# Seven block products for eight in six of ten projections, with 1024-token blocks and a second stage read back from DRAM

## The chip, the cores and the metric

The kernel runs on one core of one Trainium2 chip. Its engines work side by side, each on its own queue of instructions in a fixed order: PE (matmuls, with its weight loads shown apart as PEld), DVE (elementwise work), ACT (copies, casts, activation functions), POOL (small operations and the DMAs of its own queue) and SP (which here only issues DMAs). SBUF is the memory that the engines work on, PSUM holds matmul results in eight banks of 128 x 512 float32, and DRAM holds inputs, outputs and intermediate tensors. The metric is the time of one execution in microseconds on the device; less is better.

## What is computed

One decoder block on x of 2048 tokens x 1024 channels, all float32. The normed input is projected onto nine parts, two token mixers work on them, and two branch products, gates and an output product follow. Cut to what matters:

```python
xn = rms_norm(x, g_pre)
proj = xn @ w_in      # r_x, r_z, m_x, m_z, m_o, m_i, m_f, gate_r, gate_m
u = causal_dwconv(r_x, rg_conv_w, rg_conv_b)
h_r = rg_lru(u, headwise(u, rg_w_a) + rg_b_a, headwise(u, rg_w_x) + rg_b_x, rg_lambda)
y_r = h_r * silu(r_z)
c = silu(causal_dwconv(m_x, ml_conv_w, ml_conv_b))
q, k, v = heads(c @ w_q), heads(c @ w_k) / 16, heads(m_x @ w_v)    # 4 heads of 256
h_m = sigmoid(m_o) * mlstm_chunkwise(q, k, v, i_pre, logf)         # chunks of 128 tokens
y_m = (layer_norm(h_m) * ml_norm_g + ml_skip * c) * silu(m_z)
y = sigmoid(gate_r) * (y_r @ w_branch_r) + sigmoid(gate_m) * (y_m @ w_branch_m)
out = x + rms_norm(y @ w_out, g_post)
```

The ten large products, each 2048 x 1024 x 1024, are those of r_x, r_z, m_x, m_z, m_o, gate_r, gate_m, the two branches and w_out. `rg_lru` is a linear recurrence along the tokens, and `mlstm_chunkwise` carries a 256 x 256 state from chunk to chunk.

## The kernel before

Each float32 operand is split into a high part (a cast to the matmul's narrower format, on ACT) and a low part (the difference, on DVE). Each product is the sum of three matmuls, high x high, high x low and low x high. `wtile` (lines 215 to 226) does that for a weight tile of 128 x 1024 that SP has loaded into `raw`: `whi` by line 223, `wlo` by line 225; three buffers hold each. `split` (line 250, 253) does it for 128 x 512 activations, `stage_a2` (145, 146) for the transposed input. `mm3` (232 to 234) issues the three matmuls of one 128 x 128 weight piece, and `gemm` does so for eight pieces, 24 matmuls into one PSUM bank.

The tokens are worked through in four blocks of 512. `stage_a` loads and norms a block of x and `stage_a2` transposes it on PE (line 142), so that channels lie on the partitions. `block` then runs, for each of eight channel tiles: `rx` (projection, `conv`), the recurrence's gates, `rz`, and the R branch's gate, and after them the R branch's products (`branch_mm`). Then, for each of four heads, `ogate`, the M projections (`Head.x`, `Head.z`), values and queries (`v`, `q`), and the chunks, which are placed between the matmuls of the next head's projections by hooks. The M branch's gates and products follow, then `stage_f` with w_out. Each weight is loaded and split once in each block, four times in all. Activations between the stages stay in SBUF, in a pool of 60 slots of 128 x 512 float32 (`t2k`).

The order on each engine's queue is made when the program is built: a list scheduler goes by the place in the program's text, moves up what is ready when an engine would idle by its own clock, and lets the blocks under `high_priority` go ahead, those of `wtile` by 200 places. The waits between the engines are put in afterwards. On the chip each queue then runs strictly in that order.

The lines that the prediction's steps use: 134 (scaling of x), 142 to 146 (transpose and split of x), 223 and 225 (weight split), 232 to 234 (matmuls), 258 to 265 (`conv`), 292/293 and 486/487 (silu), 307 to 334 (the recurrence), 347 (`branch_mm`), 365 to 367 (`ogate`), 509 to 515 (values), 537 to 582 (keys, weights, state split), 603 to 612 (chunk), 633 (skip scaling), 644/647 (`back`), 759 to 778 (output).

Of the kernel before, what the change touches and what calls it, by code (L numbers as in the profile page):

```python
# [13 lines left out]
P = 128  # L14
# [5 lines left out]
NK = D // P  # L20
H = 4
# [4 lines left out]
SW = 1152  # L26
# [6 lines left out]
def hybrid_kernel(ctx: ExitStack, tc: tile.TileContext, x, w_ch, w_mo, w_gate, w_q, w_k, w_v, w_out,  # L33
# [80 lines left out]
    def stage_a(b):  # L114
# [8 lines left out]
        for t in range(NT):  # L123
            for q in range(2):
                junk = t2k("junk")
                if q and b == 0:
                    nc.vector.scalar_tensor_tensor(out=junk, in0=xh[t][q], scalar=1.0 / D, in1=xh[t][q],
                                                   op0=ALU.mult, op1=ALU.mult, accum_out=ss[:, t, q:q + 1])
                else:
                    nc.scalar.activation(out=junk, in_=xh[t][q], func=AF.Square, scale=1.0 / 32.0,  # L130
                                         accum_out=ss[:, t, q:q + 1])
            rstd = rms_scale(ss[:, t, :])
            for q in range(2):
                nc.vector.tensor_scalar(out=xh[t][q], in0=xh[t][q], scalar1=rstd, scalar2=None, op0=ALU.mult)
        return xh

    def stage_a2(xh, ks=range(NK)):
        hl = []
        for k in ks:
            ps = psum()  # L140
            for t in range(NT):
                nc.tensor.transpose(ps[:, t * P:(t + 1) * P], xh[t][k // 4][:, (k % 4) * P:(k % 4 + 1) * P], ident)
            hi = t2k("xhi", F32R)
            lo = t2k("xlo", F32R)
            nc.scalar.activation(out=hi, in_=ps, func=AF.Copy, scale=vcol(V_GPRE, k))
            last = nc.vector.scalar_tensor_tensor(out=lo, in0=ps, scalar=vcol(V_GPRE, k), in1=f32(hi),
                                                  op0=ALU.mult, op1=ALU.subtract)
            hl.append((hi, lo))
        xdone[0] = last.ins
        return hl  # L150

    with tc.high_priority():
        xT = stage_a2(stage_a(0))
# [37 lines left out]
    qk_raw = []  # L191

    def late_setup():
        nc.sync.dma_start(out=gpost_t, in_=gpost)
        for h in range(H):
            q2 = t2k("q2")
            k2 = t2k("k2")
            nc.sync.dma_start(out=q2, in_=w_q[h])
            nc.sync.dma_start(out=k2, in_=w_k[h])
            qk_raw.append((q2, k2))  # L200


    def combine_qk(h):
        q2, k2 = qk_raw[h]
# [10 lines left out]
    def wtile(width, parts):  # L215
        hi = wp.tile([P, SW], F32R, tag="whi", name=nm("whi"), bufs=3)
        lo = wp.tile([P, SW], F32R, tag="wlo", name=nm("wlo"), bufs=3)
        raw = wp.tile([P, 1056], F32, tag="raw", name=nm("raw"), bufs=RAWB)
        nw[0] += 1
        with tc.high_priority(offset=WPRI if nw[0] > 3 else 0):  # L220
            for dst, src in parts(raw):
                nc.sync.dma_start(out=dst, in_=src)
            nc.scalar.copy(out=hi[:, :width], in_=raw[:, :width])  # L223
            eng = nc.gpsimd if 1 < nw[0] < 4 else nc.vector
            eng.tensor_tensor(out=lo[:, :width], in0=raw[:, :width], in1=f32(hi)[:, :width], op=ALU.subtract)  # L225
        return hi, lo

    def wchan(i):
        return wtile(1024, lambda r: [(r[:, :1024], w_ch[i])])

    def mm3(ps, lt, rt, first, last):
        mmul(ps, lt[0], rt[0], start=first, stop=False)  # L232
        mmul(ps, lt[0], rt[1], start=False, stop=False)  # L233
        mmul(ps, lt[1], rt[0], start=False, stop=last)  # L234

    def gemm(i, rhs, hooks=None):
        whi, wlo = wchan(i)
        ps = psum()
        for k in range(NK):
# [645 lines left out]
```

## Time and profile before

| | us |
|---|---|
| median of 3 runs | 2118.42 (2117.47 to 2119.43) |
| the profiled execution | 2117.8 |
| its span, first to last instruction | 2116.0 |
| granted PE clock over it | 0.999 |

A row of a group reads: line, engine, operation, output<-inputs with sizes, count | busy us, mean ns of one | idle time of the engine just before them and what ended it. A row of the waits reads: who waited for whom: us in total, times, longest. A row of the timeline reads: start, duration, engine, line, operation. A row of the windows reads: from:to, length, then busy us (and count) of PE, PEld, DVE, ACT and POOL, granted clock, the DMA engines' share, GB/s. A row of the DMA issues ends with count, size of one and the median time from issue to landing. The slices of busy tenths, each 52.9 us, over the whole span:

```profile
PE   7999999999999999999999999999999999999998
PEld 5888899888888889988888888998888888999887
DVE  6567587856467748885546775887545677588653
ACT  4567355434356635553335754555333584455432
POOL 2010000000110100000011000000001100000000
```

The four blocks are seen as four repeats of ten slices in the row of DVE.

### The profile page before, as it was taken

Reading aid. Unit: us, or ns where it says so; the run is one execution under the profiler, and the core shown is the slowest. Engines: PE = TensorE matmul, PEld = TensorE weight load, DVE = VectorE, ACT = ScalarE, POOL = GpSimd, SP = SyncE. Lnnn points to the kernel's source line nnn. Section 1 sums busy time; section 2 is a strip of 40 time slices with the busy share of each in tenths; the row PEclk is TensorE's granted clock in tenths of the full one; section 3 lists DMA queues with packets and bytes.
Section 4 is the critical chain, followed back from the end, with each engine's and each line's share of the span. In section 5 each row is a group of like instructions: output and inputs, shape, how many; then the busy total and the mean of one; then the engine's idle time right before and its main releaser. Section 6 shows DMA issues by size and latency. Waiting matters only on the chain.

```text
span 2116.0 us, 28070 instructions
## 1 busy us (share of the span) xinstructions
PE 2089.7 (99%) x10880; PEld 1792.1 (85%) x10880; DVE 1397.2 (66%) x2323; ACT 1032.8 (49%) x1683; POOL 162.5 (8%) x318
## 2 busy tenths in 40 slices
PE   7999999999999999999999999999999999999998
PEld 5888899888888889988888888998888888999887
DVE  6567587856467748885546775887545677588653
ACT  4567355434356635553335754555333584455432
POOL 2010000000110100000011000000001100000000
PEclk9999999999999999999999999999999999999999
DMA  5322322232343232223234233222324422322223
GB/s 198 100 101 88 117 70 80 80 120 90 118 151 103 92 107 81 70 77 124 89 130 154 86 100 100 72 78 70 131 92 131 149 88 97 100 71 80 80 90 119
DMA packets 82133, 215.57 MB, mean 102 GB/s; under 512 B 8112, under 2 KB 28848, under 8 KB 82000
## 3 DMA queue, kind: packets, MB, share of 16 engines
q1 hardware_dynamic: 77968, 202.01, 29.3%
q0 software_dynamic: 3744, 11.64, 1.6%
q8 instruction: 85, 1.39, 0.3%
q14 instruction: 48, 0.39, 0.1%
q10 hardware_dynamic: 288, 0.13, 0.0%
HBM read 204.28 MB, written 9.47 MB: 101 GB/s over the span
## 4 chain that ended last, share of the span: by engine, by line
PE 95%; DVE 2%; issue 1%; ACT 1%; DMA 1%; POOL 0%; DVEq 0%; SPq 0%; POOLq 0%
PE ps L232 24%; PE ps L233 24%; PE ps L234 24%; PE ps L366 3%; PE ps L365 3%; PE ps L367 3%; PE ps L770 3%; PE ps L771 3%; PE ps L772 3%; PE ps L563 1%; PE ps L511 1%; PE ps L510 1%; PE ps L509 1%; PE ps L642 1%; PE ps L547 1%
## 5 line engine op out<-in xcount | busy, mean ns | idle before, releaser
L225 DVE TENSOR_TENSOR wlo<-raw,whi 128x1024 fp32r<-128x1024 f32 x334 | 408.7, 1224 | 378.1 <-ACT whi L223 376.9
L223 ACT CAST whi<-raw 128x1024 fp32r<-128x1024 f32 (+1 forms) x336 | 352.6, 1049 | 591.3 <-PE ps L233 255.1
L232 PE MATMUL ps<-xhi,whi 128*128 128x512 f32 x1536 | 600.0, 391 | 0.0
L233 PE MATMUL ps<-xlo,whi 128*128 128x512 f32 x1536 | 598.8, 390 | 0.0
L234 PE MATMUL ps<-xhi,wlo 128*128 128x512 f32 x1536 | 598.5, 390 | 0.0
L234 PEld LDWEIGHTS ps<-xhi,wlo 128*128 128x128 f32 x1536 | 288.5, 188 | 60.8
L232 PEld LDWEIGHTS ps<-xhi,whi 128*128 128x128 f32 x1536 | 288.8, 188 | 56.1
L233 PEld LDWEIGHTS ps<-xlo,whi 128*128 128x128 f32 x1536 | 288.7, 188 | 55.7
L265 DVE SCALAR_TENSOR_TENSOR u<-cv,vecs,u 128x512 f32<-128x512 f32 x192 | 143.9, 749 | 5.3
L365 PE MATMUL ps<-whi,xhi 128*128 128x256 f32 (+1 forms) x512 | 146.9, 287 | 0.0
L367 PE MATMUL ps<-whi,xlo 128*128 128x256 f32 (+1 forms) x512 | 145.4, 284 | 0.0
L366 PE MATMUL ps<-wlo,xhi 128*128 128x256 f32 (+1 forms) x512 | 145.0, 283 | 0.0
L347 DVE SCALAR_TENSOR_TENSOR tg<-tg,ps 128x512 f32<-128x512 f32 x64 | 43.8, 685 | 100.0 <-PE ps L234 100.0
L232 PE MATMUL ps<-yrh,whi 128*128 128x512 f32 x256 | 101.3, 396 | 0.9 <-ACT yrh L250 0.9
L233 PE MATMUL ps<-yrl,whi 128*128 128x512 f32 x256 | 100.0, 391 | 0.7 <-DVE yrl L253 0.7
L232 PE MATMUL ps<-ymh,whi 128*128 128x512 f32 x256 | 100.4, 392 | 0.0
L770 PE MATMUL ps<-whi,yh 128*128 128x512 f32 x256 | 99.9, 390 | 0.0
L234 PE MATMUL ps<-yrh,wlo 128*128 128x512 f32 x256 | 99.8, 390 | 0.0
L234 PE MATMUL ps<-ymh,wlo 128*128 128x512 f32 x256 | 99.7, 390 | 0.0
L772 PE MATMUL ps<-whi,yl 128*128 128x512 f32 x256 | 99.6, 389 | 0.0
L233 PE MATMUL ps<-yml,whi 128*128 128x512 f32 x256 | 99.6, 389 | 0.0
L771 PE MATMUL ps<-wlo,yh 128*128 128x512 f32 x256 | 99.6, 389 | 0.0
(227 smaller groups left out, 3566.7 us busy)
## 6 DMA issues: line engine op xcount, KB each, us to landing
raw<-in_w_ch_dram SPq DMA_DIRECT2D x256, 512.0 KB, 3.5
raw<-in_w_out_dram SPq DMA_DIRECT2D x32, 512.0 KB, 3.4
raw<-in_w_mo_dram SPq DMA_DIRECT2D x24, 512.0 KB, 3.9
xh<-in_x_dram SPq DMA_DIRECT2D x32, 256.0 KB, 5.8
xr<-in_x_dram SPq DMA_DIRECT2D x32, 256.0 KB, 4.2
out_dram<-o POOLq DMA_DIRECT2D x24, 256.0 KB, 3.2
raw<-in_w_mo_dram SPq DMA_DIRECT2D x8, 528.0 KB, 3.4
graw<-in_w_gate_dram SPq DMA_DIRECT2D x16, 256.0 KB, 3.7
```

Of the source, the lines that this page charges most:

```text
L223: nc.scalar.copy(out=hi[:, :width], in_=raw[:, :width])
L225: eng.tensor_tensor(out=lo[:, :width], in0=raw[:, :width], in1=f32(hi)[:, :width], op=ALU.subtract)
L232: mmul(ps, lt[0], rt[0], start=first, stop=False)
L233: mmul(ps, lt[0], rt[1], start=False, stop=False)
L234: mmul(ps, lt[1], rt[0], start=False, stop=last)
L265: nc.vector.scalar_tensor_tensor(out=u, in0=cv[:, q:q + 512], scalar=vcol(wbase + q, j), in1=u, op0=ALU.mult, op1=ALU.add)
L365: mmul(o, xh[:, sl], whi[:, ws], start=ki == 0, stop=False)
L366: mmul(o, xh[:, sl], wlo[:, ws], start=False, stop=False)
L367: mmul(o, xl[:, sl], whi[:, ws], start=False, stop=ki == NK - 1)
L770: mmul(pt, y[ki][0][:, s], whi[:, ws], start=ki == 0, stop=False)
L771: mmul(pt, y[ki][0][:, s], wlo[:, ws], start=False, stop=False)
L772: mmul(pt, y[ki][1][:, s], whi[:, ws], start=False, stop=ki == NK - 1)
```

## The change

**Seven products for eight.** For the six projections that read x (r_x, r_z, gate_r, m_x, m_z, gate_m) the kernel now works on superblocks of 1024 tokens. x is cut in two along the tokens and in two along the contraction (a11, a12, a21, a22, each 512 x 512), and a pair of channel tiles with the same halves of the contraction forms b11, b12, b21, b22. The seven products are, with s1 = a21 + a22, s2 = s1 - a11, s3 = a11 - a21, s4 = a12 - s2: a11 b11, a12 b21, s4 b22, a22 (b21 - (b22 - (b12 - b11))), s1 (b12 - b11), s2 (b22 - (b12 - b11)), s3 (b22 - b12). Products are accumulated in PSUM where their sums allow it; three sums of a pair are made by DVE out of a bank and a copy. A pair's third and fourth product run after the first four of the next pair.

**X.** `build_first` and `build_second` make seven split sets of x, of 4 x 2 slots each, 56 slots of a pool of 74. Both run at the start of the kernel for superblock 0; for superblock 1 they run at the end of the second stage of superblock 0.

**Weights.** Tiles are 128 x 512 now, in four buffers each for whi and wlo and six raw ones. The R branch loads its weights once for two blocks.

**Two stages.** `phase_a` runs, for p = 0 to 3, the six pairs of the projections, the recurrence, and two o gates of head p (one for each block). It writes yr, mx, c, mz, the branch gates gr and gm, and th to DRAM by POOL's queue. `phase_b` reads them back by SP's queue, splits yr, ym, mx and c there, and runs the heads, the branches and w_out, with hooks for the chunks in the R and M branches; the chunks of the last two heads stand ahead of half of w_out for the first block. ym and the R branch's result go through DRAM too.

**Small parts.** `conv` takes the three columns of the block before by five small POOL operations and one small addition on DVE, its first term moves to ACT; the skip scaling moves to ACT; the last block's output no longer goes tile by tile behind PE, and its stores go by POOL's queue; the memory reserved for POOL's DMA descriptors is 4096 bytes a partition.

The diff, cut to its core:

```diff
-SW = 1152
+SW = 576
+KH = NK // 2
+    def build_second(xh1, raw, X):
+        for kk in range(KH):
+            a11, a12 = raw["a11", kk], raw["a12", kk]
+            a21 = xraw(xh1, kk, "a21")
+            a22 = xraw(xh1, kk + KH, "a22")
+            X["a22"].append(split(a22, "a22"))
+            s1 = t2k("s1r")
+            tt = nc.vector.tensor_tensor
+            tt(out=s1, in0=a21, in1=a22, op=ALU.add)
+            X["s1"].append(split(s1, "s1"))
+            tt(out=s1, in0=s1, in1=a11, op=ALU.subtract)
+            X["s2"].append(split(s1, "s2"))
+            tt(out=a21, in0=a11, in1=a21, op=ALU.subtract)
+            X["s3"].append(split(a21, "s3"))
+            tt(out=a12, in0=a12, in1=s1, op=ALU.subtract)
+            X["s4"].append(split(a12, "s4"))
...
+    with tc.high_priority():
+        raw0 = build_first(load_norm(0), XS)
+        build_second(load_norm(1), raw0, XS)
...
+    def early():
+        nw[0] += 1
+        return tc.high_priority(offset=WPRI if nw[0] > 2 else 0)
+    class Pair:
...
+            with early():
+                b11 = wraw(512, w_ch[n1][:, 0:512])
+                b21 = wraw(512, w_ch[n1][:, 512:1024])
+                b12 = wraw(512, w_ch[n2][:, 0:512])
+                b22 = wraw(512, w_ch[n2][:, 512:1024])
+                f = slice(0, 512)
+                W[1] = wsplit(b11, 512)
+                W[2] = wsplit(b21, 512)
+                tt(out=b11[:, f], in0=b12[:, f], in1=b11[:, f], op=ALU.subtract)
+                W[5] = wsplit(b11, 512)
+                tt(out=b11[:, f], in0=b22[:, f], in1=b11[:, f], op=ALU.subtract)
+                W[6] = wsplit(b11, 512)
+                tt(out=b12[:, f], in0=b22[:, f], in1=b12[:, f], op=ALU.subtract)
+                W[7] = wsplit(b12, 512)
+                W[3] = wsplit(b22, 512)
+                tt(out=b21[:, f], in0=b21[:, f], in1=b11[:, f], op=ALU.subtract)
+                W[4] = wsplit(b21, 512)
+        def a(self):
+            self.x_ = psum()
+            self.prod(self.x_, 1, "a11", True)
+            m1 = t2k("m1")
+            nc.scalar.copy(out=m1, in_=self.x_)
+            z = psum()
+            self.prod(z, 2, "a12", True)
+            self.cons.add(0, 0, z, m1)
+            self.y_ = psum()
+            self.prod(self.y_, 5, "s1", True)
+            self.m5 = t2k("m5")
+            nc.scalar.copy(out=self.m5, in_=self.y_)
+            self.prod(self.x_, 6, "s2", False)
+            self.v = t2k("v")
+            nc.scalar.copy(out=self.v, in_=self.x_)
+        def b(self):
+            self.prod(self.x_, 7, "s3", False)
+            self.cons.add(1, 1, self.x_, self.m5)
+        def c(self):
+            self.prod(self.y_, 3, "s4", False)
+            self.cons.add(0, 1, self.y_, self.v)
+            self.prod(self.x_, 4, "a22", False)
+            self.cons.plain(1, 0, self.x_)
...
+    def gemm(i, ys, hooks=None):
+        ps = [psum() for _ in ys]
+        for c in range(2):
+            whi, wlo = wload(512, w_ch[i][:, c * 512:(c + 1) * 512])
+            for kk in range(KH):
+                k = c * KH + kk
+                s = slice(kk * P, (kk + 1) * P)
+                for n in range(len(ys)):
+                    mm3(ps[n], (whi[:, s], wlo[:, s]), ys[n][k], k == 0, k == NK - 1)
+                if hooks and k in hooks:
+                    hooks[k]()
...
+                pr = Pair(g, p, X, cons)
+                pr.a()
+                d, defer[:] = list(defer), []
+                if prev:
+                    prev.c()
+                for f in d:
+                    f()
+                pr.b()
+                prev = pr
...
+        for u in range(8):
+            b, h = 2 * sb + u // 4, u % 4
+            hd.s1(G)
...
+            if u < 4:
+                hd.s2()
+                for m in range(2):
+                    br(2 * h + m, hooks[m])
+            elif u < 6:
+                if u == 4:
+                    st["ym"] = loads(Q["ym"][0], "ym")
+                    st["y"] = []
+                hd.s2()
+                for m in range(4):
+                    bm(0, 4 * (u - 4) + m, {3: lambda m=m: hd.chunk(m)})
+            else:
+                hd.s2()
+                for c in range(NT):
+                    hd.chunk(c)
+                out_half(2 * sb, st["y"], u - 6, st)
+            hd.norm()
...
-NSLOT = 60
-RAWB = 3
+NSLOT = 74
+RAWB = 6
-VEB = 1
+WB = 4
```

More of the change, by code (lines that the diff above doesn't have):

```diff
@@ L135, in stage_a, with split @@
         return xh
[L137 to L150, printed above, removed]
+    def split(src, name, eng="a"):
+        hi = t2k(name + "h", F32R)
+        lo = t2k(name + "l", F32R)
+        nc.scalar.copy(out=hi, in_=src)
+        nc.vector.tensor_tensor(out=lo, in0=src, in1=f32(hi), op=ALU.subtract)
+        return hi, lo
@@ L212, in combine_qk @@
         nc.gpsimd.dma_start(out=gq_d[h], in_=g2)
[L215 to L218, printed above, removed]
-        nw[0] += 1
[L220 to L226, printed above, removed]
@@ L228, in wchan @@
-    def wchan(i):
-        return wtile(1024, lambda r: [(r[:, :1024], w_ch[i])])
-    def mm3(ps, lt, rt, first, last):
[L232 to L239, printed above, removed]
-            sl = slice(k * P, (k + 1) * P)
-            mm3(ps, (whi[:, sl], wlo[:, sl]), rhs[k], k == 0, k == NK - 1)
-            if hooks and k in hooks:
-                hooks[k]()
-        return ps
@@ new lines, in wsplit, with wload @@
+    def wsplit(raw, width):
+        hi = wp.tile([P, SW], F32R, tag="whi", name=nm("whi"), bufs=WB)
+        lo = wp.tile([P, SW], F32R, tag="wlo", name=nm("wlo"), bufs=WB)
+        nc.scalar.copy(out=hi[:, :width], in_=raw[:, :width])
+        nc.vector.tensor_tensor(out=lo[:, :width], in0=raw[:, :width], in1=f32(hi)[:, :width], op=ALU.subtract)
+        return hi, lo
+    def early():
+        nw[0] += 1
+        return tc.high_priority(offset=WPRI if nw[0] > 2 else 0)
+    def wload(width, src):
+        with early():
+            return wsplit(wraw(width, src), width)
@@ L518, in q @@
             chl = self.chl
-            whi, wlo = self.wqv
             self.qs = []
@@ new lines, in branch, with fetch, loads @@
+    def branch(i, d, ys, tgs, dsts):
+        def fetch(src, name):
+            t = t2k(name)
+            nc.sync.dma_start(out=t, in_=src)
+            return t
+        with early():
+            tg = [fetch(s, "tgl") for s in tgs]
+        pb = gemm(i + d, ys, dsts.get("hooks"))
+        for n, t in enumerate(tg):
+            nc.vector.scalar_tensor_tensor(out=t, in0=t, scalar=1.0, in1=pb[n], op0=ALU.add, op1=ALU.mult)
+        return tg
+    def loads(src, name):
+        out_ = []
+        for k in range(NK):
+            t = t2k(name)
+            with early():
+                nc.sync.dma_start(out=t, in_=src[k])
+            out_.append(split(t, name))
+        return out_
```

620 lines of the change are left out of this document (328 added, 292 removed).

## The prediction

> **What bounds the kernel now.** I read the page first: busy shares, slices, the chain, the costliest groups.
>
> ```profile
> span 2116.0 us, 28070 instructions
> PE 2089.7 (99%) x10880; PEld 1792.1 (85%) x10880; DVE 1397.2 (66%) x2323; ACT 1032.8 (49%) x1683; POOL 162.5 (8%) x318
> PE 95%; DVE 2%; issue 1%; ACT 1%; DMA 1%; POOL 0%; DVEq 0%; SPq 0%; POOLq 0%
> L225 DVE TENSOR_TENSOR wlo<-raw,whi 128x1024 fp32r<-128x1024 f32 x334 | 408.7, 1224 | 378.1 <-ACT whi L223 376.9
> L223 ACT CAST whi<-raw 128x1024 fp32r<-128x1024 f32 (+1 forms) x336 | 352.6, 1049 | 591.3 <-PE ps L233 255.1
> ```
>
> PE works through 99% of the span and carries 95% of the chain. ACT's weight cast idles 255.1 us until PE gives a weight buffer back: the preparation waits for PE, not PE for it. The waits of PE alone confirm that; the columns are total us, times, longest:
>
> ```profile
> PE ps L142 <- DVE xh L134: 17.2, 6, 12.2
> PE ps L232 <- ACT yrh L250: 0.9, 3, 0.3
> PE ps L233 <- DVE yrl L253: 0.7, 3, 0.2
> ```
>
> Outside the transposes of x (L142) PE loses 1.6 us. A busy PE need not be at its peak, so I take its pace from the timeline, start to start:
>
> ```profile
> 599.74 0.39 PE L232 MATMUL ps<-xhi,whi 128*128 128x512 f32 x1
> ...
> 605.86 0.39 PE L232 MATMUL ps<-xhi,whi 128*128 128x512 f32 x1
> ```
>
> 27 steps lie between these rows: 6.12/27 = 0.2267 us for 512 columns, not the 0.39 of one record. Only fewer matmuls shorten this kernel, and that is what the change offers.
>
> **What goes.** Six projections are 6 x 8 channel tiles x 4 token blocks x 8 x 3 = 4608 matmuls. After: 48 pairs of seven products of 4 x 3 = 84, or 4032. The 576 that go are worth 576 x 0.2267 = **130.6 us**. No other matmul goes: the four remaining products keep their terms.
>
> **What is added on DVE**, by the nearest durations:
>
> ```profile
> L253 DVE TENSOR_TENSOR cl<-u,ch 128x512 fp32r<-128x512 f32 x32 | 21.9, 685 | 5.4 <-ACT ch L250 5.4
> L134 DVE TENSOR_SCALAR xh<-xh,rstd 128x512 f32<-128x512 f32 x32 | 18.1, 613 | 4.7 <-POOL rstd L88 4.7
> L265 DVE SCALAR_TENSOR_TENSOR u<-cv,vecs,u 128x512 f32<-128x512 f32 x192 | 143.9, 749 | 5.3
> L331 DVE TENSOR_TENSOR_SCAN hr<-a,hst,u 128x512 f32<-128x512 f32 x32 | 40.9, 1278 | 0.0
> L603 DVE SCALAR_TENSOR_TENSOR cst<-cst,dec,ps 128x258 f32<-128x258 f32 x120 | 53.2, 477 | 0.0
> L250 ACT CAST ch<-u 128x512 fp32r<-128x512 f32 x32 | 19.8, 619 | 16.1 <-DVE u L479 12.3 <-DVE lf L391 3.8
> L262 DVE TENSOR_SCALAR u<-cv,vecs 128x512 f32<-128x512 f32 x64 | 34.8, 543 | 0.7 <-ACT cv L259 0.7
> L146 DVE SCALAR_TENSOR_TENSOR xlo<-ps,vecs,xhi 128x512 fp32r<-128x512 f32 x32 | 22.2, 739 | 0.0
> L633 DVE TENSOR_SCALAR u<-u,sk 128x512 f32<-128x512 f32 x32 | 14.6, 479 | 0.0
> ```
>
> A 512-column half costs 0.685, more than half of 1.224. Projection weights: 48 pairs x 11 (seven splits, four differences) x 0.685 = 361.7 in place of 192 x 1.224 = 235.0, so +127. Three sums a pair: 144 x 0.685 = +99. The R branch loads its weights for two blocks at once: 32 halves for 32 whole tiles, 21.9 - 39.2 = -17. The other 112 whole tiles become 224 halves, +16, and the o gate forms 16 differences, +11. X: 2 x 44 operations x 0.685 = 60.3 for 23.6, +37. A convolution loses the 0.543 and gains a short add (0.16 as the small rows go): 64 x -0.38 = -25. The skip scaling moves to ACT, -15; half the gate-weight splits go, -6. Sum +227: 1397 + 227 = 1624 us of a span near 2070, 78%. ACT gains 144 copies and 24 more casts and copies of X a superblock at about 0.6, some 130 us: 1033 to about 1170, 56%. Neither is the bound on average, so I charge neither in full; PE's matmuls hide them. It is the stages that decide.
>
> First stage, one p: six pairs x 84 x 0.2267, two o gates and four recurrences' gates on PE. An o gate's matmul takes 0.12 us start to start (24 steps in 2.88):
>
> ```profile
> 783.08 0.28 PE L365 MATMUL ps<-whi,xhi 128*128 128x256 f32 x1
> ...
> 785.96 0.28 PE L365 MATMUL ps<-whi,xhi 128*128 128x256 f32 x1
> ```
>
> PE 114.3 + 2 x 96 x 0.12 + 24 x 0.2267 = 142.7. DVE: 84 operations in the pairs 57.5; eight convolutions at 3 x 0.75 + 0.16, 19.3; u splits 2.7; four gates at 3.33 with the scan, 13.4; silu work 10.9; o gates 6.9; gate weights 0.7: 111, or **78%**.
>
> Second stage, one superblock: eight heads of DVE 27.8 each (from the same kinds of rows: splits 5.5, keys 1.9, state splits 2.8, weights and queries 4.1, chunks 4.1, state 3.8, norm 2.7, back 2.9), 222; R branch 33; M branch 16 x 3.43 = 55; ym 11; output 45; gate scalars 14: 380. PE: heads 8 x 19.3, R 87, M 87, output 87 = 415. That is **92%**, and where the next X is built, 40 more, 420 of about 422. The stage nearest to it in the trace is the head loop of before:
>
> ```profile
> 310.00:500.00 190.00, 189.37 (x1067) 165.60 (x1066) 139.81 (x260) 90.64 (x171) 10.87 (x24) 1.00 0.28 92
> 850.00:865.00 15.00, 15.00 (x88) 13.27 (x87) 14.06 (x31) 6.53 (x13) 1.89 (x6) 1.00 0.21 70
> ```
>
> The third number is PE, then weight loads, DVE, ACT. There PE was full with DVE at 74% over 190 us and at 94% over 15 us. (Durations overstate by the overlap of neighbours, so my 92% is rather 85 to 90.)
>
> **Waits that are added.** (a) *Weight ring.* Before, three buffers of 24 matmuls (5.44 us each). After, four of 12 (2.72 us), and W3, W4 of a pair stay parked until the next pair has run its products 1, 2, 5, 6: two rotate. From release to the next use: cast 0.62, difference 0.69, hand-overs, drain 0.17, about 1.6 of 2.72 us, where before two buffers, 10.9 us, lay ahead. Behind a late cast stand the evacuations on ACT, behind a late difference the sums on DVE. Below: 0, as PE's waits of before. Above: two more operations ahead of each, 1.3 us on half of 336 products, 220 us. (b) *Slots.* X holds 56 of 74; 18 remain for the recurrence, whose three late u with their splits, gates, copies and stores come to about 18 when the R gate's pair ends. I take **25 us** for (a) and (b), three a p: the scheduler of before left PE 1.6, so it lies near the lower end. (c) *DRAM.* ym, yr, mx, c, z, th and the branch gates now go out on POOL's queue and back on SP's:
>
> ```profile
> raw<-gq_d SPq DMA_DIRECT2D x16, 256.0 KB, 3.1
> gq_d<-g POOLq DMA_DIRECT2D x4, 256.0 KB, 2.7
> ```
>
> 2.7 + 3.1 + a split of 1.3 is 7.1 us for a tile that is wanted at once. Early loads hide most; the last head's ym before the M branch, yr at the start of the stage and the slots for the next head do not all hide, with DVE at its 92%. Between 0 and 16 heads x 7.1 = 114 I take **40 us**, some 2.5 a head, below the middle, as before hid the same path for gq_d. SP's loads stand behind weight loads that wait for a raw buffer. In bytes, 2 x 288 tiles add 151 MB and the weights lose 59: about 150 GB/s; the 405 in the last column below, from the start of before, shows the room.
>
> ```profile
> 20.00:22.70 2.70, 2.42 (x12) 2.42 (x13) 2.70 (x5) 2.46 (x5) 0.00 (x0) 1.00 1.01 405
> 22.70:24.20 1.50, 1.50 (x6) 1.27 (x6) 1.50 (x4) 0.96 (x2) 0.00 (x0) 1.00 0.60 232
> ```
>
> **Ends.** Start: before, PE ran dense from 24.1.
>
> ```profile
> 12.19 3.83 PE L142 MATMUL ps<-ident,xh 128*128 128x128 f32 x16 [12.19 <-DVE xh L134]
> 22.75 0.78 PE L232 MATMUL ps<-xhi,whi 128*128 128x512 f32 x1
> 24.11 0.40 PE L232 MATMUL ps<-xhi,whi 128*128 128x512 f32 x1
> 15.16 5.06 DVE L134 TENSOR_SCALAR xh<-xh,rstd 128x512 f32<-128x512 f32 x2
> 14.29 3.16 POOL L225 TENSOR_TENSOR wlo<-raw,whi 128x1024 fp32r<-128x1024 f32 x1 [1.73 <-ACT whi L223]
> ```
>
> Two blocks of x must land, and 36 DVE operations of the second build (25 us) follow the second. That ends near 49 us; until then PE does products 1, 2 and part of 5, 6, 7 (11.5 us): dense as if from 37, **+14** (0 to 25). End: all four banks finish together; DVE's four rounds of 2.1 us no longer hide behind PE, and the stores leave by POOL: **+5** (3 to 8).
>
> ```profile
> 2108.51 0.60 ACT L777 ACTIVATE junk<-ps 128x512 f32<-128x512 f32 x1 [2.03 <-PE ps L772]
> 2110.96 1.41 DVE L759 SCALAR_TENSOR_TENSOR o<-o,rstd,xr 128x512 f32<-128x512 f32 x2 [0.66 <-POOL rstd L88]
> ```
>
> **Sum** against the profiled run, 2117.8 us (span 2116.0, the median of three is 2118.4): 2117.8 - 130.6 + 25 + 40 + 14 + 5 = **2071 us**, -2.2%.
>
> **Rivals.** *The stalls stay hidden*, as nearly all did before: 2117.8 - 130.6 + 19 = 2006. For it: PE's 1.6 us. Against it: every margin shrank. *DRAM is late at each head* (114 for 40): 2145, slower. For it: 92% on DVE and slots that are all taken. (After the start's idle PE's first three steps took 1.36 us in place of 0.68, so each such gap may cost 0.7 more, 11 us in all: 2156. The Trainium skill, page "TensorE: Matmul & The Clock Gate", section "Why this matters for your kernels", warns of a halved clock after gaps of over about 3 us. The granted clock stood at 1.00 in those steps, row 22.70 above, so the trace does not bear the mechanism out, and no weight is on it here.) *The weight ring starves PE*, on the other side: the place is the split ahead of each of the 336 products, the price up to 220 for 25, 2266. It decides from (130.6 - 19 - 40)/336 = 0.21 us a product. For it: ACT sat idle 255 us at this very cast and blocked what stood behind it; against it: 1.1 us of slack. *POOL holds DVE up:*
>
> ```profile
> L258 POOL COPY cv<-halo x64: 180/187/1167, 5.1 to 1909.5; 128x3 f32<-128x3 f32 x64
> ```
>
> A copy of three columns takes 187 ns as a median but up to 1167 (minimum, median, maximum), and DVE's L134 above took 5.06 us for two, at 0.61 a piece elsewhere, beside POOL's 3.16. The change makes six POOL operations of two in each of 64 convolutions: 256 x 0.19 = 49 us if each stops DVE and DVE is the bound, 2120, no change. The Trainium skill, page "SBUF — State Buffer", section "Who interferes with whom", says that a DVE instruction with two SBUF inputs contends with a GpSimd instruction that reads SBUF, whoever is first blocking the other; nearly all new DVE work is of that form. These rows agree. By that rule alone the 49 us would be the price; I give it little, since at 78% DVE in that stage has room.
>
> That the change does less than it says can't be: the matmuls are counted off the loops.
>
> **Chances.** Forecast (2025 to 2110) 0.45; hidden 0.20; DRAM 0.10; ring 0.14; POOL 0.05; 0.06 in between, mostly above. Faster by over 0.2%: 0.66; within 0.2%, about what a measurement of this kernel can tell from no change: 0.05; slower: 0.29. Eight in ten: below 2003 I leave 0.05, above 2190 some 0.14.
>
> **What would show it.** Right: 10304 matmuls, DVE near 1600 us or less by its page sum, PE's spacing unchanged at 0.227, PE idle near 100 us in all (ends included). Gaps of PE ahead of products, released by wlo or whi, are (a); ahead of ym, yr or mx splits, or behind DMA, (c); ahead of X's splits at the first 50 us, the start. The DVE share of the second stage against 92% tests the table. The prediction is wrong if PE's idle time exceeds 130 us or one of the stages runs at DVE's pace.

## The result, and the profile after

The changed kernel takes 2499.19 us (median of 4, 2496.11 to 2500.39) against 2118.49 for the one before: a ratio of **1.1795 [1.1775, 1.1815]**, 18% slower where 2.2% faster was forecast. The profiled execution took 2496.1 us. Its page, the busy times:

```profile
span 2494.3 us, 30483 instructions
PE 2094.7 (84%) x10304; PEld 1746.7 (70%) x10304; DVE 1608.4 (64%) x2941; ACT 1194.2 (48%) x2183; POOL 507.5 (20%) x868
```

The 576 matmuls are gone, and DVE (1608 us, forecast 1624) and ACT (1194, forecast 1170) carry what was worked out. Neither of the two got a larger share than forecast (64% for 78%, 48% for 56%): PE got emptier, from 99% to 84%, and its clock slower, from a mean of 0.999 to 0.917. The waits of PE (who waited for whom: us in total, times, longest) say where:

```profile
PE ps L258 <- DVE z L323: 114.2, 24, 17.7
PE ps L258 <- ACT ymh L137: 50.6, 10, 13.4
PE ps L571 <- DVE ex L564: 43.8, 4, 19.4
PE ps L646 <- ACT mxh L137: 32.4, 9, 6.6
...
PE ps L258 <- issue: 19.4, 6, 4.4
PE ps L258 <- ACT tr L435: 17.4, 7, 2.5
...
PE ps L495 <- ACT whi L245: 6.7, 7, 1.2
```

All rows of this view sum to 385.6 us, where before they summed to 18.8. Without any new loss the profiled run would have been 2117.8 - 130.6 = 1987.2, so 508.9 us were lost: 367 of them are waits by this view, and some 142 are the half clock and short waits that it doesn't name. PE's busy time bears that out: 2094.7 where 2089.7 - 130.6 = 1959.1 was due, 135.6 more. Three windows show the stages (from:to, length, then busy us and count of PE, PEld, DVE, ACT and POOL, granted clock, DMA share, GB/s): the first stage of the second superblock, then the two second stages, cut at the first matmul of each:

```profile
1290.95:1967.14 676.19, 600.07 (x2892) 500.76 (x2890) 443.88 (x721) 356.27 (x582) 198.69 (x322) 0.94 0.30 103
747.98:1290.95 542.97, 443.80 (x2246) 369.22 (x2247) 359.32 (x745) 238.31 (x506) 50.28 (x94) 0.90 0.44 150
1967.14:2481.66 514.52, 426.60 (x2182) 358.23 (x2182) 327.11 (x676) 207.40 (x440) 45.23 (x85) 0.91 0.45 151
```

The forecast's table had 571 us of PE for four p's and 415 for a second stage. So this first stage lost 105 us and the second stages 128 (with the next x's transposes) and 100, though DVE was busy there for only 66% and 64% of the time.

Of the waits, those for weights (last row) hardly count; z is the largest. It is the sum (1,1) of R's Z pair, which DVE must make out of PE's bank before product 4 may add to that bank. First a window in one such wait:

```profile
490.00:500.00 10.00, 0.55 (x3) 0.12 (x1) 5.58 (x7) 7.33 (x9) 0.96 (x1) 0.65 0.07 26
```

Then DVE's timeline in it (start, duration, line, operation; in brackets how long it waited and for whom):

```profile
491.00 0.69 DVE L246 TENSOR_TENSOR wlo<-raw,whi 128x512 fp32r<-128x512 f32 x1 [2.64 <-ACT whi L245]
492.15 0.69 DVE L450 SCALAR_TENSOR_TENSOR w<-aq,tr 128x512 f32<-128x512 f32 x1 [0.45 <-ACT aq L449]
494.03 0.69 DVE L450 SCALAR_TENSOR_TENSOR w<-aq,tr 128x512 f32<-128x512 f32 x1 [1.19 <-ACT aq L449]
496.50 1.29 DVE L454 TENSOR_TENSOR u<-w,u 128x512 f32<-128x512 f32 x2 [1.77 <-ACT w L452]
497.71 2.45 DVE L456 TENSOR_TENSOR_SCAN hr<-a,hst,u 128x512 f32<-128x512 f32 x2
500.08 0.66 DVE L323 TENSOR_TENSOR z<-ps,m 128x512 f32<-128x512 f32 x1
```

In these 10 us PE is busy 0.55, DVE 5.58, ACT 7.33. DVE is not full; it stands still four times, three times for ACT's part of the recurrence (L449 and L452) and once, 2.64 us, for a weight cast that stands among that part in ACT's queue. z stands behind all of it in DVE's queue, although PE began the last matmul into its bank (product 7) at 474.92. When PE resumes, its steps have twice the length, as its timeline shows:

```profile
500.80 0.79 PE L258 MATMUL ps<-a22h,whi 128*128 128x512 f32 x1 [10.24 <-DVE z L323]
...
505.23 0.63 PE L260 MATMUL ps<-s2h,wlo 128*128 128x512 f32 x1
505.65 0.63 PE L258 MATMUL ps<-s2h,whi 128*128 128x512 f32 x1
...
507.02 0.40 PE L259 MATMUL ps<-s2l,whi 128*128 128x512 f32 x1
507.26 0.39 PE L260 MATMUL ps<-s2h,wlo 128*128 128x512 f32 x1
```

0.42 or 0.43 us from start to start up to 506.5, then 0.23 or 0.24: the granted clock is 0.50 from 500.8 to 506.4, and PE pays after the stall too.

DVE's timeline at the joint of the two stages:

```profile
768.06 9.19 DVE L138 TENSOR_TENSOR yrl<-yr,yrh 128x512 fp32r<-128x512 f32 x14 [1.52 <-ACT yrh L137]
777.16 0.67 DVE L543 TENSOR_REDUCE am<-ar 4x4 f32<-4x512 f32 x1
...
779.73 0.15 DVE L564 TENSOR_TENSOR ex<-eye,mlst 4x16 f32<-4x16 f32 x1
```

And PE's, which waits for the last of these:

```profile
779.94 0.63 PE L571 MATMUL ps<-ex,ones 4*128 4x32 f32 x2 [19.37 <-DVE ex L564]
```

The gate scalars, under 3 us of small operations, stand behind fourteen splits of yr. A part of the 19.37 us is the reload of yr: ACT's casts ahead of those splits wait 3.63, 1.59 and 0.15 us for it. What ACT waits in all for two other reloads of the second stage:

```profile
ACT ymh L137 <- DMA ym<-dym: 41.6, 14, 11.2
ACT mxh L137 <- DMA mxr<-dmx: 31.3, 18, 3.4
```

At one of the waits for ymh, which begins at 1158.30, SP issues the first of these reloads only when PE stands still already, behind loads of x for the output (from 1156.5 on):

```profile
1161.61 3.83 SPq L849 DMA_DIRECT2D ym<-dym  x5
1168.86 0.62 ACT L137 CAST ymh<-ym 128x512 fp32r<-128x512 f32 x1 [9.03 <-DMA ym<-dym]
1169.53 0.79 PE L258 MATMUL ps<-ymh,whi 128*128 128x512 f32 x1 [11.23 <-ACT ymh L137]
```

### The profile page after: what moved, and what is told of

The parts are those of the page before. It is cut to its first block, busy times and chain, and to the rows that moved or that the text cites. A ratio compares the mean times of both kernels' runs of the same rounds, so it can differ in the third digit from the quotient of the medians.

```text
span 2494.3 us, 30483 instructions
## 1 busy us (share of the span) xinstructions
PE 2094.7 (84%) x10304; PEld 1746.7 (70%) x10304; DVE 1608.4 (64%) x2941; ACT 1194.2 (48%) x2183; POOL 507.5 (20%) x868
## 5 line engine op out<-in xcount | busy, mean ns | idle before, releaser
L245 ACT CAST whi<-raw 128x512 fp32r<-128x512 f32 (+1 forms) x592 | 366.7, 620 | 658.2 <-PE ps L259 409.1
L246 DVE TENSOR_TENSOR wlo<-raw,whi 128x512 fp32r<-128x512 f32 (+1 forms) x592 | 406.7, 688 | 384.4 <-ACT whi L245 377.4
L258 PE MATMUL ps<-a22h,whi 128*128 128x512 f32 x192 | 82.8, 431 | 114.2 <-DVE z L323 114.2
L339 DVE SCALAR_TENSOR_TENSOR u<-xq,vecs,u 128x511 f32<-128x511 f32 (+2 forms) x192 | 143.7, 749 | 14.4 <-ACT u L337 10.8
L258 PE MATMUL ps<-ymh,whi 128*128 128x512 f32 x256 | 103.1, 418 | 51.5 <-ACT ymh L137 50.6
L258 PE MATMUL ps<-s1h,whi 128*128 128x512 f32 x192 | 80.2, 418 | 31.3 <-ACT tr L435 17.4
L258 PE MATMUL ps<-s2h,whi 128*128 128x512 f32 x192 | 83.4, 434 | 11.4 <-ACT m L300 11.4
L259 PE MATMUL ps<-s2l,whi 128*128 128x512 f32 x192 | 81.3, 423 | 0.0
L260 PE MATMUL ps<-s2h,wlo 128*128 128x512 f32 x192 | 80.2, 418 | 0.0
L259 PE MATMUL ps<-s1l,whi 128*128 128x512 f32 x192 | 79.5, 414 | 0.2 <-DVE s1l L138 0.2
L259 PE MATMUL ps<-a22l,whi 128*128 128x512 f32 x192 | 79.2, 412 | 0.0
```

The costliest lines, as they stand in the source:

```text
L246: nc.vector.tensor_tensor(out=lo[:, :width], in0=raw[:, :width], in1=f32(hi)[:, :width], op=ALU.subtract)
L258: mmul(ps, lt[0], rt[0], start=first, stop=False, skip_group_check=True)
L259: mmul(ps, lt[0], rt[1], start=False, stop=False, skip_group_check=True)
L260: mmul(ps, lt[1], rt[0], start=False, stop=last, skip_group_check=True)
L339: nc.vector.scalar_tensor_tensor(out=u[:, s:], in0=xq[:, :512 - s], scalar=vcol(wbase + 3 - s, j), in1=u[:, s:], op0=ALU.mult, op1=ALU.add)
```

## The experiments

My first theory was the forecast's own (b) and (c), mis-sized: slots and the hand-over through DRAM. Rivals were the weight ring (a), DVE's load, and the order of work in the queues: operations that PE needs next stand behind others that wait. All ratios are to the kernel before, which ran on the same chip. Where an edit adds or removes lines, the line numbers of a row are off by one to four.

### Slots, ring, hand-over: e1 to e4

e1_a22 frees eight slots (product 4 reads a12 in a22's place, four splits fewer in each superblock):

```diff
-            X["a22"].append(split(a22, "a22"))
+            X["a22"].append(X["a12"][kk])
```

> The set a22 is not split any more; its product reads the tiles of a12, so 8 of the 56 slots of X are free and 26 are left for everything else (that product's result is another). Slots theory: in the first stage the wait of some 10 us of the fourth product on the bank sum z, and the one of 2.5 us on the gates, both seen once a p, shrink to little: 8 x (12.7 + about 4 of slow clock) = 134 us less, about 2365. Weight-ring theory: only 8 splits less in each superblock, 2490 or so. The order of the second stage keeps its own waits under both.

e2_order puts the pair of gate_m ahead of r_z's:

```diff
-            steps = [RX, GR, RZ, MX, GM, MZ]
+            steps = [RX, GR, GM, RZ, MX, MZ]
```

> The same work, with the six pairs of a p in the order RX, GR, GM, RZ, MX, MZ: a second gate pair, which holds few slots, stands between the recurrence's gates and the pair RZ that needs slots for its sums. Slots theory: the slots' demand is spread, the 10 us wait per p shrinks by half or more, 2380 to 2450. Ring theory, or DVE as the bound: the same splits and the same sums, 2490 to 2510.

e3_ym feeds the M branch with mz, written long before, in place of ym:

```diff
-                    st["ym"] = loads(Q["ym"][0], "ym")
+                    st["ym"] = loads(Q["mz"][0], "ym")
```

> The second stage reads the mz tiles, written long before, where it read ym (so the M branch's product is another); the work is the same and only the dependence on data written a moment ago goes. Hand-over theory (the trip out and back is too late): the waits for ymh, 50.6 us on PE in all and up to 13.4 each, go, with some slow clock behind them: about 2435. If the loads are late because no slot is free or because they stand late in the queue, nothing changes: 2490 to 2505.

e4_ring5 gives the ring a fifth buffer, paid for by narrower tiles and an unused pad (not shown):

```diff
-SW = 576
+SW = 528
-WB = 4
+WB = 5
```

> Five whi and five wlo buffers for four (the room comes from tiles 528 for 576 wide and the unused pad). Ring theory: a second product is prepared ahead, the first stage loses most of its waits, 2300 to 2400. Slots theory: within 15 us of 2499.

Measured: e1 2489.43 us (1.1753 [1.1719, 1.1788]), e2 2476.32 (1.1692 [1.1658, 1.1725]), e3 2497.6 (1.1792 [1.1758, 1.1826]), e4 2508.02 (1.1841 [1.1807, 1.1876]). With eight more slots (e1) the waits on z come to 114.2 us in 24, as in the changed kernel.

So neither slots nor ring nor the age of ym is the main cause: e1 came out where the ring's theory had put it, but e4, which tests the ring itself, is no faster, and in e3 ymh still costs 49.2 us. e2, which only moves a pair, does more than any of them, and lies between its two ranges (z 107.4). What remained was the theory of order.

### What holds z up: e5, e6, e9, e10, e11

e5_zfirst moves product 7 and its sum ahead of the deferred gates:

```diff
+                pr.b()
                 for f in d:
                     f()
-                pr.b()
```

> In the first stage each pair's product 7 and its sum (1,1) stand ahead of the recurrence's gates of the pair before, in place of behind them; the same instructions, another place in the text. Order theory (the bank sum z is late because it stands behind the recurrence's operations on DVE's queue, whose inputs ACT makes late): the eight waits of product 4 on z, 10.2 to 17.7 us each, 114 us in all, fall below 40 us, with the slow clock behind them and part of the waits on tr: 2360 to 2420 us, ratio 1.12 to 1.14. Load theory (DVE or ACT has too much to do in that stretch, whatever the order): the waits move to other products, and the time stays within 2470 to 2510 us.

Measured 2502.59 us (1.1818 [1.1784, 1.1852]): not in the range of the order theory but in that of the load theory. In PE's waits z shrank, and others came in its place:

```profile
PE ps L258 <- ACT m L300: 53.6, 9, 8.0
...
PE ps L495 <- ACT whi L245: 33.0, 7, 5.2
PE ps L258 <- DVE z L323: 24.1, 16, 11.7
```

Another operation stands behind the gates now, and PE waits for that. Order or load, this run doesn't tell; e10 and e11 do. e6_notable takes ACT's table loads out of the recurrence:

```diff
-                nc.scalar.activation(out=tt, in_=pg, func=AF.Sigmoid, ...
+                nc.scalar.activation(out=tt, in_=pg, func=AF.Abs, ...
-            nc.scalar.activation(out=w2, in_=w2, func=AF.Sqrt, bias=tiny_t)
+            nc.scalar.activation(out=w2, in_=w2, func=AF.Square, bias=tiny_t)
```

> The gates' Sigmoid becomes Abs and the Sqrt of w2 becomes Square, so the recurrence's numbers are others; the operations, their shapes and their order in the text stay, but ACT's table loads of 1.28 us ahead of them (about 56 of them, 72 us of ACT) should go. Table theory (the order was made without the table loads, which make ACT's chain of gates later on the chip than the order supposes): the waits of product 4 on z fall from 114 us to under 60, and the time to 2400 to 2450 us. Order theory without the tables (the chain is long and stands ahead of z in any case): z's waits stay over 85 us and the time is 2460 to 2500 us.

Measured 2447.44 us (1.1557 [1.1524, 1.1591]), z at 94.9. The changed kernel's groups of table loads on ACT, 56 in these four rows (busy us, mean ns):

```profile
L435 ACT ACT_TABLE_LOAD x16 | 20.5, 1283 | 0.3
L446 ACT ACT_TABLE_LOAD x16 | 20.5, 1283 | 0.3
L452 ACT ACT_TABLE_LOAD x16 | 20.5, 1283 | 0.3
L397 ACT ACT_TABLE_LOAD x8 | 10.3, 1283 | 4.5 <-DVE z L323 4.4
```

71.8 us went off an ACT that is busy 48% of the time, and 52 of them came off the total: here the length of ACT's chain counts, not its load. (The Trainium skill, page "ScalarE: Activation LUTs", section "What ACT_TABLE_LOAD costs", gives about 1283 ns for a load; the rows agree.) z fell less than that theory asked (under 60), so the tables are a part.

e9_fresh starts products 6, 7, 3 and 4 in banks of their own:

```diff
-            self.prod(self.x_, 7, "s3", False)
+            self.x_ = psum()
+            self.prod(self.x_, 7, "s3", True)
```

> Products 6, 7, 3 and 4 of a pair each start a fresh PSUM bank in place of adding to the bank that an earlier product filled; that leaves out the sums of the seven products, and the operations, their counts and their places stay. Coupling theory (PE waits because a product that accumulates cannot start until ACT's copy or DVE's sum has read that bank, and that reader stands late in its queue): product 4 no longer waits on z, and the 114 us on z fall below 30 without coming back elsewhere, 2350 to 2420 us. Burst theory (the recurrence's operations hold DVE and ACT up, so whatever needs them is late, banks and weights too): the waits move to the weights or to a bank's release, 2470 to 2510 us.

The sums of the seven products are left out by it. Measured 2449.54 us (1.1562 [1.1518, 1.1607]), between the two ranges. In its waits PE meets z now at the o gate (here L499), which needs a bank:

```profile
PE ps L499 <- DVE z L327: 37.4, 7, 5.4
```

So the accumulation in PSUM, which ties PE's next product to a reader on DVE or ACT, is worth up to 50 us, and the late readers do harm without it too.

e10_spread issues at most two deferred pieces in a step. The text of the changed kernel puts three of a p's four gates, and so both of its chains of two, into the step of r_z.

```diff
-                d, defer[:] = list(defer), []
+                d, defer[:] = defer[:2], defer[2:]
```

> Of the deferred pieces (the recurrence's gates and output products) at most two are issued in a step of the first stage, in place of all that wait; the same work, spread over three or four steps. Burst theory: the 114 us on z and the 17 us on tr fall by a third to two thirds, the time to 2400 to 2460 us. Coupling theory: the chain of one pair of gates is still ahead of a bank's reader, so the waits only change place, 2480 to 2520 us.

Measured **2403.41 us** (1.1345 [1.1312, 1.1378]), 96 less, in the burst theory's range. z falls to 31.6, and the waits of the second stage stay (ymh 51.0, ex 43.3, mxh 33.5). One p as a window of the changed kernel, from one product 4 that waited to the next p's:

```profile
1392.07:1555.74 163.67, 149.15 (x721) 124.82 (x721) 110.75 (x201) 87.50 (x145) 49.32 (x80) 0.95 0.29 99
```

And one p of e10, from one wait on tr to the next:

```profile
1343.12:1493.30 150.18, 146.66 (x721) 123.03 (x721) 109.56 (x201) 86.89 (x145) 49.36 (x80) 0.99 0.33 108
```

The same 721 matmuls, 201 and 145 operations, in 13.5 us less. The kernel before shows that it isn't the load: in a window of nearly that length PE was full beside as much work on DVE and more on ACT:

```profile
600.00:760.00 160.00, 159.48 (x759) 133.19 (x758) 111.71 (x169) 96.83 (x133) 17.50 (x32) 1.00 0.35 113
```

Its `block` ran one gate and one finish (the scan) for each channel tile, in separate places. e11_nowlo turns the question round and takes load off DVE:

```diff
-        nc.vector.tensor_tensor(out=lo[:, :width], in0=raw[:, :width], in1=f32(hi)[:, :width], op=ALU.subtract)
-        return hi, lo
+        return hi, hi
```

> The low part of every weight tile is left out (the high part is used in its place), which takes 592 DVE operations of 0.688 us, 407 us, a quarter of DVE's work, and one hand-over ahead of each weight; PE and ACT do what they did. Load theory (DVE is the bound in the stretches that stall): idle time of PE falls by more than half, 2200 to 2300 us. Order and latency theory (PE waits for chains of hand-overs that stand in a fixed order, not for DVE's throughput): 2400 to 2480 us, with the waits on ex, ymh and mxh within 20% of 44, 51 and 32 us.

Its page, the busy times:

```profile
PE 2075.8 (85%) x10304; PEld 1740.4 (72%) x10304; DVE 1241.6 (51%) x2349; ACT 1198.3 (49%) x2183; POOL 452.1 (19%) x868
```

Measured 2433.63 us (1.1487 [1.1454, 1.1521]). 367 us of DVE's work went and 66 came off the total, with the waits on z at 111.0, ymh 46.4, ex 42.4 and mxh 28.3, as the theory of order and latency had it: DVE's throughput isn't the bound.

### The second stage: e7, e8, e12, e13, e14, e18

```diff
 e7_gates: yr's loads behind the gate scalars and the first head's v and q
-        yr = [loads(Q["yr"][bi], "yr") for bi in range(2)]
-        hd.v(); G.part2(); hd.q(); G.part3()
+        G.part2(); hd.v(); G.part3(); hd.q()
+        yr = [loads(Q["yr"][bi], "yr") for bi in range(2)]
 e8_queue: in Head and loads
-                nc.sync.dma_start(out=t, in_=src)
+                nc.gpsimd.dma_start(out=t, in_=src)
 e12_cover: the chunks go between w_out's matmuls
-                for c in range(NT):
-                    hd.chunk(c)
-                out_half(2 * sb, st["y"], u - 6, st)
+                out_half(2 * sb, st["y"], u - 6, st, {2 * c + 1: lambda c=c: hd.chunk(c) for c in range(NT)})
```

> At the start of the second stage the gate scalars (part 2 and 3) stand ahead of the loads and splits of yr in the text. Order theory: the two waits for ex of 19.4 and 19.0 us shrink to the chain's own length, some 8 us, the slow clock behind them with it: 20 to 45 us less, 2450 to 2480 us. If the chain of the gate scalars itself is what takes the time: the waits stay and the time is within 2490 to 2505 us.

> The reloads of mx, c, th, mz, yr and ym are issued from POOL's queue in place of SP's, so that they don't stand behind weight loads that wait for a raw buffer. Queue theory (ymh, mxh and yr splits are late because SP issues their loads late): the waits on ymh (50.6 us) and mxh (32.4 us) halve at least, and the time is 2420 to 2460 us. Slot theory (the loads wait for slots in any queue): the waits stay as they are, 2490 to 2510 us. If the order of ACT's and DVE's queues in that stage is what delays the splits, the loads land earlier but the waits stay within 20%.

> In the last two heads of each second stage the four chunks stand between the matmuls of w_out (after its weight tiles 1, 3, 5 and 7) in place of ahead of them all; the same work. Cover theory (at the joints between heads PE has nothing else in its queue while the chain of weights and splits runs): the four stalls of 4.6 us in that place and some of the 1.4 us beside them go, and the half clock behind them, 15 to 40 us less, 2460 to 2485 us. If DVE's and ACT's load in that stage sets the pace, they reappear in the chunks or in the next head: 2490 to 2510 us.

Measured: e7 2510.29 us (1.1854 [1.182, 1.1889]), outside both ranges, and longer: ex fell from 43.8 to 13.5, but mxh rose from 32.4 to 40.1, issue (PE waits for nothing that the profile shows) to 25.6, and yrh came in with 14.3. e8 2486.91 (1.1744 [1.171, 1.1778]): ymh 43.9, mxh 28.8, a good tenth less and not a half, and ex 32.0; the queue of the loads is a part. ACT still waits 33.9 us for the reloads of ym and 34.0 for those of mx there. e12 2479.98 (1.1706 [1.1672, 1.174]), 19 less, as expected, though ymh fell from 50.6 to 25.5 and 13.0 us of issue came elsewhere.

```diff
 e13_gatesearly, at the end of a step in phase_a
+                if p == 3 and n == 2:
+                    G = Gates(fts[0])
+                    G.part1()
+                if p == 3 and n == 3:
+                    G.part2()
+                if p == 3 and n == 4:
+                    G.part3()
 e14_ymearly, ahead of the second half of w_out
+                if u == 7:
+                    ym6 = loads(Q["ym"][1], "ym", range(6))
 e18_fewyr
-        yr = [loads(Q["yr"][bi], "yr") for bi in range(2)]
+        yr = [loads(Q["yr"][bi], "yr", (0, 1)) * 4 for bi in range(2)]
```

> The gate scalars of a superblock's first block (parts 1, 2 and 3) are made in the last three steps of the first stage, where PE has projections to do, in place of at the start of the second. Burst theory (a chain of small operations stalls PE only where it stands in line with what PE needs next): the waits on ex go from 43.8 to under 8 us, and, other than with yr moved behind them, nothing takes their place: 2440 to 2470 us. Load theory (the second stage's DVE and ACT cannot feed PE at that point): the stall comes back on yrh or mxh, 2490 to 2510 us.

> Six of the eight ym tiles of a superblock's second block, those of heads 0 to 2, are loaded and split ahead of the second half of w_out for the first block, in place of behind it. Order theory: the two stalls of 11.2 and 13.4 us ahead of the second M branch shrink below 4 us each, the half clock behind them too: 2465 to 2485 us. Slot theory (no free slots for them any earlier): 2490 to 2505 us, with the wait on ymh as before.

> At the start of the second stage only the first two yr tiles of each block are loaded and split, and each is used for four of the eight parts of the contraction; that leaves out twelve of the sixteen reloads and splits of yr there (0.6 us on ACT and 0.69 on DVE each), 24 of each in all. PE's work stays. Joint theory (between the stages the splits of yr stand in ACT's and DVE's queues ahead of what the first head needs): the waits on ex fall from 44 us to under 25, the time by 15 to 40 us, to 2460 to 2485 us. If the chain of the gate scalars takes that time by itself: the waits on ex stay over 38 us, and the time is 2490 to 2505 us.

Measured: e13 2487.06 us (1.1744 [1.1701, 1.1787]), e14 2485.37 (1.1736 [1.1701, 1.177]), e18 2482.96 (1.1725 [1.1686, 1.1765]). e13 lies between its ranges, e14 at the edge of that of order (ymh 34.9), e18 in that of the joint. In e13 the stall stayed at the joint, and PE's waits name another cause (ex 5.4):

```profile
PE ps L700 <- ACT q L664: 39.6, 10, 16.5
```

ACT's timeline there:

```profile
769.95 8.37 ACT L137 CAST yrh<-yr 128x512 fp32r<-128x512 f32 x13 [0.79 <-DMA yr<-dyr]
778.23 1.06 ACT L664 COPY q<-ps 128x512 f32<-128x512 f32 x2
```

The first head's queries wait behind 13 casts of yr on ACT, as ex waited behind them on DVE. With a quarter of the reloads and splits (e18) ex falls to 27.6, not under 25; its stall of 10.90 us at the joint still holds 4.6 us of ACT's waiting for yr's reload and the gate scalars. So it is in the main yr's preparation, reload and splits, which begins when the first stage is over and PE has nothing else to do.

### Clock and sums: e17, e15, e19

e17_filler puts 44 matmuls without use ahead of products 3 and 4 of R's Z pair:

```diff
+            if isinstance(self.cons, SiluOut) and self.cons.r:
+                dps = psum()
+                for i in range(44):
+                    mmul(dps, self.W[3][0][:, 0:P], self.X["s4"][0][0], start=i == 0, stop=i == 43)
             self.prod(self.y_, 3, "s4", False)
```

> 44 matmuls of 512 columns that nobody reads (10.0 us at 0.227) are put ahead of the product 4 that waits for z, once for each p, 352 in all, so that PE works through that wait of 10.2 to 17.7 us. Clock theory (the half clock is granted because PE idled): the wait on z shrinks to a few us, no half-clock stretch follows it, and though PE does 80 us more work the time falls by 10 to 30 us, to 2470 to 2490 us. If the half clock does not come from PE's idling: the added work hides in the wait at best, 2495 to 2505 us, and where it doesn't fit it adds up to 80 us, 2580.

Measured **2466.22 us** (1.1645 [1.1611, 1.1679]): with 352 matmuls more, 80 us of work, the kernel is 33 us shorter, a little below the clock theory's range. A p of the changed kernel (the one after that shown above) and the same p with the filler, as windows:

```profile
1555.74:1719.46 163.72, 148.87 (x720) 124.63 (x721) 106.07 (x163) 86.87 (x141) 50.13 (x80) 0.95 0.29 98
1545.33:1702.90 157.57, 154.93 (x765) 129.91 (x765) 105.58 (x164) 86.68 (x141) 49.83 (x80) 1.00 0.31 102
```

163.72 us at a clock of 0.95 against 157.57 at 1.00, with 44 matmuls (10.0 us) more. PE's idle time in the window fell from 14.85 to 2.64 us: 12.2, of which the filler took 10.0. That leaves 2.2 us from the waits, on z and on tr, that went. The other 3.9 us are PE's own: it was busy 154.93 us where 148.87 + 10.0 would be due, so the same matmuls ran faster. PE's idling causes the half clock. The order of the queues is made anew with the filler in it, but DVE's last operations ahead of z are the same. (The Trainium skill, page "TensorE: Matmul & The Clock Gate", section "Why this matters for your kernels", warns of just this for gaps of over about 3 us; the filler bears it out.) In this kernel a shorter gap did it too: after a wait of 2.48 us for tr, which ended at 485.95, the clock is halved (0.52 from 486.0 to 489.3), while after the waits of 1.08 us for z that the filler leaves it stays at 1.00.

e15_all joins e10, e12, e13 and e14 and norms both blocks of x ahead of the first transposes; e19_more adds e2 and e8 and puts yr's loads behind the first head's queries.

> Together: the deferred pieces at two a step, the chunks of the last two heads between w_out's matmuls, the gate scalars early, six ym tiles early, and both blocks of x loaded and normed ahead of the first transposes. If each is its own stall and gives what it gave alone (about 96 + 19 + 45 + 25 + 8): 2290 to 2330 us. If one load stands behind all stalls and they return elsewhere: 2360 to 2420 us. Neither is below the kernel before.

> All of the run before that put the changes together, and three more: the M branch's gate pair ahead of the Z pair of R, the reloads by POOL's queue, and yr loaded and split behind the first head's queries. If the stalls at the joints are separate chains: 23 + 12 + some 20 less than the 2377 us of that run, 2315 to 2335 us. If the joints between stages and heads have too little matmul work beside what they must prepare, wherever it stands: 2350 to 2385 us. Either way slower than the kernel before.

Measured: e15 2377.26 us (1.1225 [1.1192, 1.1258]), 122 less than the changed kernel where its parts had given 96 + 19 + 12 + 14 = 141 alone (the start wasn't tried alone). That lies in the range of the theory that one load stands behind all stalls; but the other range was built on 45 and 25 us for e13 and e14, which gave 12 and 14, and 122 of 141 speaks for stalls that are mostly separate. e19 **2312.45** (1.092 [1.0888, 1.0952]), 65 less again and 2.5 below the range for separate chains. By edits of place and queue alone 187 us came back, with the same work, but not enough: the kernel before remains the faster. What e19 still waits for, its largest rows:

```profile
PE ps L647 <- ACT mxh L137: 35.6, 8, 6.2
PE ps L259 <- DVE z L324: 29.7, 12, 11.2
```

## Why the prediction was wrong

**What held.** 10304 matmuls; DVE 1608 us for 1624; ACT 1194 for 1170; for one p 110.75 us of DVE for 111. The end: from PE's last matmul to the last instruction 12.7 us for 7.5, +5.2 for +5. Outside the half-clock stretches the spacing is 0.227 as before (11 steps from 1535.55 to 1538.05), so the 130.6 us stand.

**The step that failed** is the passage from the shares to the waits: "It is the stages that decide", followed by 78% and 92% of DVE and by 25 us for (a) and (b), "three a p". A share tells whether an engine can do its work in a stage, not whether what PE needs next stands behind something that waits. In the first stage the table was right and one p took 163.67 us for 142.7: 21 us, seven times the three. In the second stage DVE had less to do than the table said (327 us for 380, 359 for 420, so 64% and 66% for 92%), no stage ran at DVE's pace, and yet 100 and 128 us were lost. The cause in the first stage is in none of the terms. Gates and scans come bunched in one step, wait for each other across ACT and DVE, and hold readers of PSUM banks on which PE's next product depends, since the seven products add to banks that others have to read in between. Spreading the bunch gave 96 us (e10), shortening ACT's chain 52 (e6), cutting the tie to the banks 50 (e9); these overlap. In the second stage it is in the main term (c), which follows.

**(a) weight ring, (b) slots:** not the cause (e4 no faster, e1 10 us less; waits for whi at the o gate 6.7). The rival of the ring, 2266, ended on the right side by a mechanism that isn't there.

**(c) DRAM, 40 us:** the place was right, the size wasn't, and the mechanism was half right. ymh, ex and mxh come to 126.8 us of waits. Of the path that was priced at 7.1 us, out, back and split, the way out isn't what is waited for (e3, for ym), but the way back is: ACT's casts wait 41.6 us for the reloads of ym and 31.3 for those of mx. These reloads and their splits are issued in a bunch when the stage or the head begins, behind and ahead of other work, and the joints have no matmuls to cover them (e12, e13, e18). Issuing six of ym's earlier took ymh from 50.6 to 34.9 (e14). "Early loads hide most", taken over from gq_d, did not hold here.

**Start, +14:** low, and above its range of 0 to 25. In the window of the first 76 us PE is busy 33.65 us (before: 60.66), so some 27.

```profile
0.00:76.00 76.00, 33.65 (x121) 23.78 (x122) 53.31 (x112) 47.77 (x96) 13.64 (x33) 0.71 0.29 103
```

**The clock.** Put aside in brackets, "no weight is on it here", because the granted clock stood at 1.00 in three slow steps of the kernel before. That was a wrong reading: the three steps took 1.36 us in place of 0.68, twice their length, and should have been believed over the column. With many stalls it matters: mean clock 0.917, and 33 us less with useless work added (e17).

**POOL holding DVE up, 2120:** POOL is busy 507.5 us, and the five small operations of a convolution, priced at 0.19 us each, took 0.44 to 0.95. But DVE's sum is under its forecast, and the convolution's operation on DVE, which has two inputs in SBUF, took 749 ns as before; nothing of it is seen. (The row of L134, said to agree with that rule, is of an operation with one tile as input and doesn't bear on it.) **Hidden, 2006:** fell.

The stated sign of error, "PE's idle time exceeds 130 us", came true: 2494.3 - 2094.7 = 400 us.

**Open.** Whether the bunches come from the text alone or also from the scheduler's own clock, which may see shorter chains than the chip, wasn't tried. How much of the reloads' lateness comes from SP's queue, from slots and from the place in the text was not separated (e8 moved the queue alone, e14 the place of six). In e19 some 232 us of waits remain (sum of its rows); whether the joints of the heads can be covered wasn't settled.

## What to carry to other kernels

When a change takes work off a full engine, list for each step what that engine needs next, on which queue the reader or maker stands, and the longest chain that can stand ahead of it there; shares of busy time don't price that. If products accumulate into banks that others read in between, bunched side work must be spread so that no chain ahead of a reader is longer than the matmuls queued meanwhile. Price a stall with the half clock behind it (3.9 us a p here), and look at the start of each stage for preparation that nothing covers: a reload that is issued when PE runs dry comes too late by its whole way in.

## What the hardware showed unexpectedly

Useless matmuls made the kernel faster: 352 of them, 80 us, for a gain of 33 us. A stall of 10.24 us left PE at 0.42 us a step for 5.7 us more (500.80 to 506.5). And the column of the granted clock can read 1.00 over steps that run at half pace: in the kernel before PE's first product began at 22.75, and its first two steps took 0.58 and 0.42 us (the column there, 1.00, stood in the forecast; the trace has no record of the clock before 24.0).
